# A hand-written order of instructions with longer due times for data that goes through DRAM, and a reordered opening

## The chip, the cores and the metric

The kernel runs on one core of one Trainium2 chip. The metric is the device time of one execution in microseconds (us), the median over the runs. A core has five engines with a stream of instructions each: PE (TensorE, matmuls), DVE (VectorE), ACT (ScalarE), POOL (GpSimd) and SP (SyncE, which here only issues DMAs). Each engine takes its instructions in the order of its stream and stops at one whose data is not there.

## The reference

One layer of a hybrid decoder for a prompt of 512 tokens and 8 sequences of 4 tokens (544 columns in all), model width 1024. Cut to what matters:

```python
mod = silu(c) @ w_ada + b_ada                    # adaLN: six vectors of 1024 per sequence
h = rmsnorm(x, mix_pre_g) * (1 + sc_m) + sh_m
p_rw, p_cv, p_gt = split(h @ w_in)               # 59 weight columns of 128
# RWKV-7: S_t = S_{t-1} diag(w_t) + S_{t-1} (-kk_t)(kk_t*a_t)^T + v_t k_t^T ;  y_t = S_t r_t
# convolution branch: GLU, depthwise conv (31 taps), layernorm, silu, w_conv_out
merged = sigmoid(g_a) * (y * g) @ w_o_rwkv + sigmoid(g_b) * y_b
x = x + gt_m * rmsnorm(merged @ w_out)
hf = rmsnorm(x) * (1 + sc_f) + sh_f              # then router, top 6 of 64 experts, shared expert
x = x + gt_f * rmsnorm(moe(hf))
```

## The kernel before

Activations stand transposed (128 channels by 544 tokens, eight such tiles). Float32 products are made from two fp32r parts: a weight column of 1024 x 128 is loaded, split by ACT (`wh`) and DVE (`wl`), and multiplied in 48 matmuls (eight channel tiles, three products, two halves of the tokens; line 611). `Stream` runs all columns of `w_in` one after the other in an order written by hand, with the convolutions among them, and then those of the two output projections. Each column's product lies in one of two PSUM tiles; column n waits until the output step of column n−2 has emptied its tile.

Around this stream run threads, each a Python generator: the opening, one for the adaLN rows, one for preparation and Gram matrices of the eight head pairs, the inverses, their assembly, the scan, the sample states. `Weave` puts them into one order: a thread yields an engine letter with an estimated duration, and an earliest start if it has one; the planner picks the next step by estimated time and priority and then emits its instructions. Nothing else decides the order on an engine. The estimates do not act on the chip: there an instruction waits only for its data. `arrival(mb)` is the planner's estimate for a transfer: 2 us, the megabytes at 0.36 MB/us behind earlier ones, and 1.2 us.

The places that matter here:

- Opening. `th_first` issues the loads on SP: c, all constants, x in two halves, sixteen adaLN weights of 0.52 MB with six buffers, the parameters among them, and at the end 2.2 MB of zeros into the accumulator `accs[1]`. `th_ada` multiplies each weight with silu(c) (line 468) and picks the rows by a second product (511). `th_ssq` squares x on ACT and sums over channels with 32 matmuls (526), then root and reciprocal (534). `th_h` makes xn, hf, hh and hl per channel tile; column 0 follows tile by tile, later columns come after it.
- adaLN rows (`th_rows`, line 1339 on). The other 32 weights come in pairs through two buffers; four weights are multiplied per PSUM bank while the lock `L` on two banks is held, which `sample`, `assemble` and `step` also take.
- Gram matrices (`gram`). For each head pair two halves: products on PE (995, 996), mask on DVE (1001) into `gm`, of which there is one buffer, six DMAs to DRAM. The transposes behind (1018) use the PSUM banks of the products. The step in question is

```python
            yield 'V', 1.37, max(t + .2, tv[-1] + 4. if c0 else 0)
            gm = rt([128, 4, 2, 2, 64], "gm", 1)
```

- Inverses. `th_inverse` solves 31 steps on DVE, writes the blocks to DRAM; `assemble` reads them back in another layout (`d1`, `gt`, `TT`) and multiplies (1195, 1208), then the scan of eight steps follows, for each of two groups of head pairs.
- After the columns of `w_in` and the scan: `th_yin` loads what the y stage needs, `th_y` normalises, `th_z`, router, experts.

Of the kernel before, what the change touches and what calls it, by code (L numbers as in the profile page):

```python
# [10 lines left out]
FT = mybir.dt.float32  # L11
# [3 lines left out]
OP = mybir.AluOpType  # L15
# [42 lines left out]
C_ID, C_MEAN, C_BLK, C_ONE, C_TRI = 0, 128, 256, 384, 512  # L58
C_HS = 640
C_SCAN = 642  # L60
# [6 lines left out]
C_SELC = C_SELR + 64  # L67
C_E64 = C_SELC + 9
C_EPS = C_E64 + 64
C_TOK = C_EPS + 2  # L70
# [285 lines left out]
def hybrid_kernel(ctx: ExitStack, tc: tile.TileContext, a, dbg=None, stop=None):  # L356
# [103 lines left out]
    x_in, c_done, r_done = events(2), Event(), Event()  # L460
    aw = {}
# [8 lines left out]
    def th_first():  # L470
        yield 'D', .5
        t = load(cT, a['cT'], .13)
        yield 'D', .5
        load(cst, a['const'][:, :C_END], .92)
        for s in (slice(0, 4), slice(4, 8)):
            yield 'D', .5
            x_in[s.start // 4].t = load(xT[:, s], a['xT'][:, s], 1.1)
        for i in range(16):
# [17 lines left out]
        load(accs[1][NP:], zt[:NS], .13)  # L496
# [19 lines left out]
    def th_ssq():  # L516
        ps = None
# [18 lines left out]

    def th_h(q):
        yield r_done
        for j in range(q, 8, 2):
            yield a_mod[8 + j]  # L540
            yield a_mod[j]
            yield 'V', .7
            V.tensor_scalar(A1[:, j, :], modT[:, 8 + j, :], 1.0, P_(P_G1, j), op0=OP.add, op1=OP.mult)
            xn = ap_.tile([128, T], FT, name="xn", tag=f"xn{q}", bufs=1)
            V.tensor_tensor(xn, xT[:, j, :], rstd, op=OP.mult)
# [16 lines left out]
    class Stream:  # L562
# [9 lines left out]
        def split(self):  # L572
            raw, at, m = {}, {}, 0
            ns = [n for n, c in enumerate(self.cols) if c[0] is not None]
            for i, n in enumerate(ns):
                while m < min(i + 2, len(ns)):
                    yield 'S', .4
# [1931 lines left out]
```

## Time and profile before

| | us |
|---|---|
| median of 3 runs | 1701.23 (1693.86 to 1704.89) |
| the profiled execution | 1702.24 |
| its span | 1700.4 |
| PE busy | 1500.6 (88%) |
| DVE busy | 692.7 (41%) |
| ACT busy | 525.8 (31%) |
| mean granted TensorE clock | 0.959 of full speed |

The page is read from the top: busy time of each engine, then the span in 40 slices, the chain of work that ended last, and the costliest groups of instructions with the idle time before them and what ended it. A busy PE is not PE at its peak. Idle time of an engine matters only where that engine sets the end of a stage, so the views are read stage by stage: busy times in windows, waits in a window, and the timeline.

### The profile page before, as it was taken

The numbers are of one execution on the slowest core, as the hardware profiler recorded it, in microseconds if no ns is written. First come the engines' busy times: TensorE is split into PE (matmuls) and PEld (weight loads), VectorE is DVE, ScalarE is ACT, GpSimd is POOL, SyncE is SP. The second block draws the span as 40 slices with busy tenths as digits, with TensorE's granted clock in tenths as the row PEclk, the third lists the DMA queues.
The fourth block names the chain that finished last, engine by engine and source line by source line (L and its number), as shares of the span: only waits on it lengthen the run. The fifth ranks groups of instructions, "written<-read, shape, count | busy, mean of one in ns | idle before, by whom it ended". The sixth has DMA issues, their size and how long they took to land.

```text
span 1700.4 us, 31359 instructions
## 1 busy us (share of the span) xinstructions
PE 1500.6 (88%) x12550; PEld 1071.6 (63%) x12550; DVE 692.7 (41%) x1633; ACT 525.8 (31%) x994; POOL 183.2 (11%) x171
## 2 busy tenths in 40 slices
PE   6889998988899987999999999999888898889891
PEld 4778777877787777998997774545433343333330
DVE  3527463577576675854553431212211111111113
ACT  4334342442354423561323512212111111111112
POOL 0000000000000000000000011223222222222211
PEclk9989999999799998999999999999999999999995
DMA  9786676558688687647625259999999999999997
GB/s 351 250 243 181 194 190 167 129 138 193 135 207 203 156 208 185 175 144 216 220 86 175 87 204 380 352 343 318 333 343 343 355 353 355 350 351 369 349 379 218
DMA packets 212328, 421.89 MB, mean 248 GB/s; under 512 B 95702, under 2 KB 135510, under 8 KB 186966
## 3 DMA queue, kind: packets, MB, share of 16 engines
q1 hardware_dynamic: 183926, 344.29, 62.5%
q10 hardware_dynamic: 17136, 46.60, 9.2%
q0 software_dynamic: 11120, 28.99, 7.4%
q8 instruction: 99, 1.62, 0.4%
q14 instruction: 47, 0.39, 0.1%
HBM read 359.20 MB, written 68.35 MB: 251 GB/s over the span
## 4 chain that ended last, share of the span: by engine, by line
PE 42%; issue 22%; DMA 15%; DVE 7%; POOL 6%; ACT 3%; SPq 3%; POOLq 0%; ACTq 0%; DVEq 0%
PE mm L611 18%; POOL acc L2192 3%; POOL xg L2187 3%; PE z L1631 3%; PE gu L2261 3%; PE ye L2268 2%; DMA wr<-in_w_in 2%; DMA im<-in_w_ada 2%; PE mm L805 2%; PE gu L2258 2%; DMA acc<-yo,tok 2%; DMA raw<-in_w_ex 2%; DMA imd<-gm 1%; SPq L445 1%; PE yt L1576 1%
## 5 line engine op out<-in xcount | busy, mean ns | idle before, releaser
L611 PE MATMUL mm<-hh,wh 128*128 128x272 f32 x944 | 224.6, 320 | 3.2 <-DVE gt L650 2.8
L611 PE MATMUL mm<-hl,wh 128*128 128x272 f32 x944 | 201.5, 296 | 0.8 <-DVE hl L556 0.8
L611 PE MATMUL mm<-hh,wl 128*128 128x272 f32 x944 | 200.2, 294 | 0.4 <-DVE wl L588 0.4
L611 PEld LDWEIGHTS mm<-hh,wh 128*128 128x128 f32 x944 | 155.2, 197 | 23.3 <-issue 17.1
L2261 PE MATMUL gu<-raw,xs 128*48 128x256 f32 (+2 forms) x1248 | 148.4, 386 | 22.6 <-DMA raw<-in_w_ex 18.9
L2304 DVE SCALAR_TENSOR_TENSOR hs<-hs,gate,gu 64x256 f32<-64x256 f32 (+6 forms) x65 | 30.7, 473 | 320.6 <-ACT hs L2302 320.6
L2268 PE MATMUL ye<-raw,ht 128*48 128x512 f32 (+6 forms) x440 | 139.8, 614 | 18.5 <-ACT ht L2311 15.0
L611 PEld LDWEIGHTS mm<-hl,wh 128*128 128x128 f32 x944 | 154.6, 196 | 1.3 <-DVE hl L556 1.2
L611 PEld LDWEIGHTS mm<-hh,wl 128*128 128x128 f32 x944 | 153.6, 196 | 0.7 <-DVE wl L588 0.7
L2258 PE MATMUL gu<-raw,xs 128*80 128x512 f32 (+3 forms) x304 | 136.4, 599 | 7.8 <-DMA raw<-in_w_ex 6.0
L2261 PEld LDWEIGHTS gu<-raw,xs 128*48 128x48 f32 (+2 forms) x1248 | 78.6, 125 | 92.9 <-DMA raw<-in_w_ex 25.1
L2192 POOL DMA_INDIRECT acc<-yo,tok x65 | 91.9, 1414 | 292.7 <-ACT yo L2331 253.1
L588 DVE TENSOR_TENSOR wl<-wr,wh 128x1024 fp32r<-128x1024 f32 x75 | 91.5, 1220 | 75.0 <-ACT wh L586 75.0
L2328 DVE COPY yo<-ye 64x512 f32<-64x512 f32 (+6 forms) x65 | 44.4, 684 | 185.6 <-PE ye L2268 165.4
L2302 ACT ACTIVATE hs<-gu 64x256 f32<-64x256 f32 (+6 forms) x65 | 24.7, 380 | 262.4 <-PE gu L2258 135.0
L2331 ACT ACTIVATE yo<-ye 64x512 f32<-64x512 f32 (+6 forms) x65 | 38.5, 593 | 213.1 <-DVE yo L2328 210.4
L2258 PEld LDWEIGHTS gu<-raw,xs 128*80 128x80 f32 (+3 forms) x304 | 48.4, 165 | 85.0 <-issue 68.2
L586 ACT ACTIVATE wh<-wr 128x1024 fp32r<-128x1024 f32 x75 | 79.5, 1059 | 50.8 <-PE mm L611 37.5
L2187 POOL DMA_INDIRECT xg<-td,tok x65 | 72.0, 1108 | 201.7 <-PE xgT L2247 187.2
L2268 PEld LDWEIGHTS ye<-raw,ht 128*48 128x48 f32 (+6 forms) x440 | 39.5, 139 | 78.6 <-issue 53.8
L805 PE MATMUL mm<-g,wdw 128*32 128x256 f32 x1024 | 58.6, 381 | 2.8 <-ACT dw L820 2.8
L1405 POOL MEMSET im<- 64x256 f32 x2 | 0.6, 307 | 495.2 <-DMA g<-gcd 327.7
(415 smaller groups left out, 2434.6 us busy)
## 6 DMA issues: line engine op xcount, KB each, us to landing
raw<-in_w_ex SPq DMA_DIRECT2D x168, 1024.0 KB, 9.8
wr<-in_w_in ACTq DMA_DIRECT2D x59, 512.0 KB, 5.2
tT<-in_w_ex SPq DMA_DIRECT2D x24, 1024.0 KB, 9.6
im<-in_w_ada SPq DMA_DIRECT2D x16, 1024.0 KB, 8.7
im<-imd SPq DMA_DIRECT2D x32, 512.0 KB, 6.9
g<-gcd SPq DMA_DIRECT2D x64, 142.0 KB, 5.3
aw<-in_w_ada SPq DMA_DIRECT2D x16, 512.0 KB, 5.6
gated<-gt ACTq DMA_DIRECT2D x16, 272.0 KB, 2.1
```

Of the source, the lines that this page charges most:

```text
L586: S.activation(hi, raw[i], AF.Copy)
L588: V.tensor_tensor(lo, raw[i], hi, op=OP.subtract)
L611: PE.matmul(ps[:, h, :H2], w[:, k, :], x[:, k, h * H2:(h + 1) * H2], start=(k == 0 and i == 0), stop=(k == KT - 1 and i == 2))
L805: PE.matmul(ps[32 * g:32 * g + 32, c, :256], w[:, b, g], x[:, g, 4 * b:4 * b + 256], start=(b == 0), stop=(b == 7))
L1631: PE.matmul(ps[:, h], m[:, k, OFF[tt]:OFF[tt] + 128], WO[w][:, k, 512 * h:512 * h + 512], start=(k == 0 and n == 0), stop=(k == KT - 1 and ...
L2187: G.indirect_dma_start(out=xg[:n], out_offset=None, in_=td, in_offset=bass.IndirectOffsetOnAxis(ap=col, axis=0), bounds_check=T - 1, oob_i ...
L2192: G.indirect_dma_start(out=accs[i], out_offset=bass.IndirectOffsetOnAxis(ap=col, axis=0), in_=ye[:n], in_offset=None, bounds_check=T - 1, ...
L2258: PE.matmul(pg[:n], x[:, k, :n], w, start=(k == 0), stop=(k == KT - 1))
L2261: PE.matmul(pg[p:p + n, :256], x[:, k, :n], w[:, c:c + 256], start=(k == 0), stop=(k == KT - 1))
L2268: PE.matmul(py[h], x[:, k, :n], w[:, 1024 * k + 512 * h:1024 * k + 512 * h + 512], start=(k == 0), stop=(k == 1))
L2328: V.tensor_copy(ye[:n, :512], py[0])
L2331: S.activation(ye[:n, 512:], py[1], AF.Copy)
```

## The change

Constants are laid out anew so that those of the opening (mean matrix, selection, epsilon) stand first; they are loaded alone, the rest after the tenth adaLN weight. The opening loads c and x first. Squares are made on ACT as before, but summed on DVE, and one product per half follows; xn is made in place on DVE in a thread of its own. The first two columns run together, tile by tile as h comes, each with its own PSUM tile; their output steps start when the opening's memory is released. The zeros go into the y stage, their memset from POOL to DVE. The planner's due times: second Gram mask 9 instead of 4 us after the first, assembly 6 us after the estimated arrival, row weights 3.5 us after it, with 0.65 instead of 0.85 us per product; loads of the first two column weights not before 14 us.

```diff
-C_ID, C_MEAN, C_BLK, C_ONE, C_TRI = 0, 128, 256, 384, 512
+C_MEAN, C_SELC, C_EPS, C_EARLY = 0, 128, 137, 144
+C_ID, C_BLK, C_ONE, C_TRI = (C_EARLY + 128 * i for i in range(4))
...
     def th_first():
         yield 'D', .5
         t = load(cT, a['cT'], .13)
-        yield 'D', .5
-        load(cst, a['const'][:, :C_END], .92)
         for s in (slice(0, 4), slice(4, 8)):
             yield 'D', .5
             x_in[s.start // 4].t = load(xT[:, s], a['xT'][:, s], 1.1)
+        yield 'D', .5
+        cst_in.t = load(cst[:, :C_EARLY], a['const'][:, :C_EARLY], .07)
+        yield 'D', .5
+        load(par, a['par'], .19)
+        W.spawn('first', th_silu(t), 4)
         for i in range(16):
...
             a_in[i].t = load(aw[i], a['w_ada'][AORD[i]], .52)
-            if i == 0:
-                yield 'S', .3, t
-                S.activation(cs, cT, AF.Silu)
-                fire(c_done)
-            if i == 1:
+            if i == 9:
                 yield 'D', .5
-                load(par, a['par'], .19)
-        zt = ap_.tile([128, D], FT, name="zeros")
-        yield 'G', .6
-        G.memset(zt, 0.0)
-        yield 'D', 1.
-        load(accs[1][:NP].rearrange("(i p) d -> p i d", p=128), zt[:, None].to_broadcast([128, 4, D]), 2.1)
-        load(accs[1][NP:], zt[:NS], .13)
+                load(cst[:, C_EARLY:], a['const'][:, C_EARLY:C_END], .85)
...
+    def th_sq():
         for j in range(8):
             yield x_in[j // 4]
-            yield 'S', .55
-            sq = ap_.tile([128, T], FT, name="sq", tag="sq", bufs=2)
-            S.activation(sq, xT[:, j, :], AF.Square)
-            yield 'P', .9
-            ps = ps or [bank([128, H2], "ssq") for _ in range(2)]
-            for h in range(2):
-                PE.matmul(ps[h], C_(C_MEAN, 128), sq[:, h * H2:(h + 1) * H2], start=(j == 0), stop=(j == 7))
+            yield 'S', .6
+            sqs[j] = ap_.tile([128, T], FT, name="sq", tag="sq" if j else "sum", bufs=3 if j else 1)
+            S.activation(sqs[j], xT[:, j, :], AF.Square)
+            fire(sq_in[j])
+
+    def th_ssq():
+        for j in range(8):
+            yield sq_in[j]
+            if j:
+                yield 'V', .72
+                V.tensor_tensor(sqs[0], sqs[0], sqs[j], op=OP.add)
...
+    def th_xn():
+        yield r_done
+        for j in range(8):
+            yield 'V', .72
+            V.tensor_tensor(xT[:, j], xT[:, j], rstd, op=OP.mult)
+            fire(xn_in[j])
...
                 while m < min(i + 2, len(ns)):
-                    yield 'S', .4
+                    yield 'S', .4, 14. if m < 2 else None
...
-                if i >= 2:
+                if i >= 3:
                     yield self.g[ns[i - 2]]
...
         def mm(self):
             for n, (src, ops, need, label, out) in enumerate(self.cols):
                 W.label(label)
+                if n == 1:
+                    continue
+                if not n:
+                    two = [n, n + 1]
+                    for i in two:
+                        yield self.s[i]
+                    ps = [mmtile() for _ in two]
+                    for k in range(KT):
+                        yield need[k]
+                        xh, xl = ops()
+                        for j in two:
+                            yield 'P', .76
...
+                    yield st_open
+                    for j in two:
+                        W.spawn(self.cols[j][3], self.cols[j][4](ps[j], self.e[j]), 3)
+                    continue
...
-            yield 'V', 1.37, max(t + .2, tv[-1] + 4. if c0 else 0)
+            yield 'V', 1.37, max(t + .2, tv[-1] + 9. if c0 else 0)
...
-        t = W.arrival(1.0)
+        t = W.arrival(1.0) + 6.
...
-                    yield 'P', .85, max(t, now())
+                    yield 'P', .65, max(t + 3.5, now())
...
         y_in.t = load(BR['XG'], xgd.rearrange("i p t -> p i t"), .56)
+        zt = yp.tile([128, D], FT, name="zeros")
+        yield 'V', 1.2
+        V.memset(zt, 0.0)
+        yield 'D', 1.
+        load(accs[1][:NP].rearrange("(i p) d -> p i d", p=128), zt[:, None].to_broadcast([128, 4, D]), 2.1)
+        load(accs[1][NP:], zt[:NS], .13)
...
-    W.run(h_done)
+    W.run([*h_done, gemms.g[1]])
```

## Rows read from the trace of the kernel before

**Rows 1.** Busy times in windows; columns: stretch, length, engines (instructions), clock, DMA share, GB/s.

```profile
58.00:740.00 682.00, 616.25 (x6918) 532.00 (x6915) 417.58 (x989) 270.91 (x508) 5.02 (x8) 0.94 0.71 180
...
775.00:900.00 125.00, 124.38 (x1069) 118.13 (x1069) 66.31 (x91) 32.24 (x37) 2.66 (x8) 0.99 0.54 168
...
1000.00:1600.00 600.00, 537.50 (x3048) 260.76 (x3046) 107.76 (x334) 114.25 (x247) 153.96 (x123) 0.99 1.01 349
```

**Rows 2.** PE's waits from 57 to 740: who waited for whom, us, times, longest.

```profile
PE bt L1018 <- DVE gm L1001: 24.4, 6, 6.9
PE pz L1195 <- DMA dx<-d1d: 15.4, 4, 7.7
PE rows L468 <- DMA im<-in_w_ada: 11.6, 5, 3.5
```

**Rows 3.** Busy times in windows after PE's stalls, and in one dense stretch.

```profile
86.10:92.30 6.20, 6.13 (x46) 4.44 (x46) 1.66 (x5) 2.55 (x5) 0.00 (x0) 0.50 1.08 232
...
440.10:454.20 14.10, 14.10 (x278) 13.16 (x280) 5.76 (x8) 1.77 (x3) 0.00 (x0) 0.50 0.42 69
...
817.00:890.00 73.00, 73.00 (x583) 72.88 (x582) 41.80 (x47) 24.97 (x27) 2.66 (x8) 1.00 0.48 155
```

**Rows 4.** PE's timeline in the first of these windows: start, us, instruction, count.

```profile
88.66 0.66 PE L611 MATMUL mm<-hl,wh 128*128 128x272 f32 x2
89.11 0.65 PE L611 MATMUL mm<-hh,wl 128*128 128x272 f32 x2
```

**Rows 5.** Timeline of the opening: reciprocal, last adaLN weight, ends of columns 0 and 1.

```profile
30.82 3.56 DVE L534 RECIPROCAL rstd<-rstd 128x272 f32<-128x272 f32 x2 [0.67 <-ACT rstd L530]
...
48.17 0.64 PE L468 MATMUL ada<-aw,cs 128*32 128x128 f32 x16
...
55.87 0.41 PE L611 MATMUL mm<-hh,wl 128*128 128x272 f32 x2
...
66.33 0.41 PE L611 MATMUL mm<-hh,wl 128*128 128x272 f32 x2
```

**Rows 6.** Busy times in a window of the opening.

```profile
4.00:30.00 26.00, 16.67 (x148) 12.16 (x152) 3.92 (x10) 9.65 (x18) 0.00 (x0) 1.00 1.02 418
```

**Rows 7.** Timeline of DVE and SP around two of eight pairs of Gram masks.

```profile
392.23 1.28 DVE L1001 TENSOR_TENSOR gm<-gram,cst 128x512 f32<-128x512 f32 x2
...
402.23 0.61 SPq L1009 DMA_DIRECT2D imd<-gm  x1
...
404.74 1.29 DVE L1001 TENSOR_TENSOR gm<-gram,cst 128x512 f32<-128x512 f32 x2 [7.45 <-DMA imd<-gm]
...
567.69 1.29 DVE L1001 TENSOR_TENSOR gm<-gram,cst 128x512 f32<-128x512 f32 x2 [0.15 <-PE gram L996]
...
575.11 1.29 DVE L1001 TENSOR_TENSOR gm<-gram,cst 128x512 f32<-128x512 f32 x2 [0.37 <-issue]
```

**Rows 8.** PE's timeline at the first assembly.

```profile
438.26 0.28 PE L1195 MATMUL pz<-dx,lx 32*32 32x32 f32 x2 [4.33 <-DMA dx<-d1d]
440.10 1.88 PE L1195 MATMUL pz<-dx,lx 32*32 32x32 f32 x62 [1.55 <-DMA dx<-d1d]
```

**Rows 9.** DMA issues from 0 to 60: count, KB each, us to landing.

```profile
acc<-zeros SPq DMA_DIRECT2D x1, 2048.0 KB, 10.3
```

**Rows 10.** DVE's timeline: a head pair's v done, its preparation's start; last Gram's end.

```profile
418.56 0.23 DVE L650 SCALAR_TENSOR_TENSOR v<-sh,par,v 128x8 f32<-128x8 f32 x1
...
420.37 0.50 DVE L890 TENSOR_SCALAR kn<-k,par 128x544 f32<-128x544 f32 x1
...
582.02 0.43 DVE L1039 TENSOR_TENSOR bonus<-half,v 128x272 f32<-128x272 f32 x1
```

**Rows 11.** Timeline at the stage's end: scan's last copy, last head norm, last gate's DMA.

```profile
737.10 0.38 ACT L1294 ACTIVATE ysb<-py 128x256 f32<-128x256 f32 x1 [2.34 <-PE py L1247]
...
755.44 0.69 DVE L1326 TENSOR_TENSOR ys<-ys,st 128x512 f32<-128x512 f32 x1
...
764.24 0.34 ACTq L690 DMA_DIRECT2D gated<-gt  x1
```

More of the change, by code (lines that the diff above doesn't have):

```diff
@@ L56 @@
 LOW = -3e38
-C_ID, C_MEAN, C_BLK, C_ONE, C_TRI = 0, 128, 256, 384, 512
-C_HS = 640
-C_SCAN = 642
+C_MEAN, C_SELC, C_EPS, C_EARLY = 0, 128, 137, 144
+C_ID, C_BLK, C_ONE, C_TRI = (C_EARLY + 128 * i for i in range(4))
+C_HS = C_TRI + 128
+C_SCAN = C_HS + 2
 C_MP = C_SCAN + T
@@ L66 @@
 C_SELR = C_LM + 1
[L67 to L70, printed above, removed]
+C_E64 = C_SELR + 64
+C_TOK = C_E64 + 64
 C_OV = C_TOK + 5
@@ L459, in hybrid_kernel @@
     a_in, a_out, a_mod, h_done = events(16), events(16), events(16), events(8)
-    x_in, c_done, r_done = events(2), Event(), Event()
-    aw = {}
+    x_in, c_done, r_done, cst_in, xn_in = events(2), Event(), Event(), Event(), events(8)
+    st_open, aw = Event(), {}
     rstd = ap_.tile([128, T], FT, name="rstd")
@@ L514, in th_ada @@
             fire(a_mod[n])
-    def th_ssq():
-        ps = None
+    sq_in, sqs = events(8), {}
+    def th_sq():
         for j in range(8):
             yield x_in[j // 4]
-            yield 'S', .55
-            sq = ap_.tile([128, T], FT, name="sq", tag="sq", bufs=2)
-            S.activation(sq, xT[:, j, :], AF.Square)
-            yield 'P', .9
-            ps = ps or [bank([128, H2], "ssq") for _ in range(2)]
-            for h in range(2):
-                PE.matmul(ps[h], C_(C_MEAN, 128), sq[:, h * H2:(h + 1) * H2], start=(j == 0), stop=(j == 7))
+            yield 'S', .6
[8 more added lines that the diff above has]
+                V.tensor_tensor(sqs[0], sqs[0], sqs[j], op=OP.add)
+        sum_ = sqs[0]
+        yield cst_in
+        yield 'P', 1.9
+        ps = [bank([128, H2], "ssq") for _ in range(2)]
+        for h in range(2):
+            PE.matmul(ps[h], C_(C_MEAN, 128), sum_[:, h * H2:(h + 1) * H2], start=True, stop=True)
         for h in range(2):
             s = slice(h * H2, (h + 1) * H2)
-            yield 'S', .4
+            yield 'S', .5, None, 'sqrt'
             S.activation(rstd[:, s], ps[h], AF.Sqrt, bias=C_(C_EPS, 1))
@@ L535, in th_ssq @@
         fire(r_done)
+    def th_xn():
[4 more added lines that the diff above has]
+            fire(xn_in[j])
     def th_h(q):
-        yield r_done
         for j in range(q, 8, 2):
+            yield xn_in[j]
             yield a_mod[8 + j]
             yield a_mod[j]
-            yield 'V', .7
+            yield 'V', .22
             V.tensor_scalar(A1[:, j, :], modT[:, 8 + j, :], 1.0, P_(P_G1, j), op0=OP.add, op1=OP.mult)
-            xn = ap_.tile([128, T], FT, name="xn", tag=f"xn{q}", bufs=1)
-            V.tensor_tensor(xn, xT[:, j, :], rstd, op=OP.mult)
+            xn = xT[:, j]
             yield 'S', .7
@@ L580, in split @@
                     m += 1
-                if i >= 2:
+                if i >= 3:
                     yield self.g[ns[i - 2]]
                 yield 'S', 1.05, at[i]
-                hi = wp.tile([128, KT, 128], FR, name="wh", tag="wh", bufs=2)
-                lo = wp.tile([128, KT, 128], FR, name="wl", tag="wl", bufs=2)
+                hi, lo = ((wp if i else ap_).tile([128, KT, 128], FR, name=w, tag=w, bufs=2 if i else 1) for w in ("wh", "wl"))
                 S.activation(hi, raw[i], AF.Copy)
@@ L594, in mm @@
                 W.label(label)
+                if n == 1:
[10 more added lines that the diff above has]
+                            yield 'P', .76
+                            wh, wl = self.hl[j]
+                            for i, (w, x) in enumerate(((wh, xh), (wh, xl), (wl, xh))):
+                                for h in range(2):
+                                    PE.matmul(ps[j][:, h, :H2], w[:, k, :], x[:, k, h * H2:(h + 1) * H2],
+                                              start=(k == 0 and i == 0), stop=(k == KT - 1 and i == 2))
+                    for j in two:
+                        fire(self.g[j])
+                    yield st_open
+                    for j in two:
+                        W.spawn(self.cols[j][3], self.cols[j][4](ps[j], self.e[j]), 3)
+                    continue
                 if src is None:
@@ L1766, in hybrid_kernel @@
         W.spawn('ada', th_ada(q), 2)
+    W.spawn('ssq', th_sq(), 4)
     W.spawn('ssq', th_ssq(), 3)
+    W.spawn('ssq', th_xn(), 0)
     for q in range(2):
@@ L1777, in hybrid_kernel @@
     cv['gg'] = cvp.tile([128, GW], FT, name="gg")
+    st_open.t = W.last
     G.memset(cv['gg'], 0.0)
```

5 lines of the change are left out of this document (4 added, 1 removed).

## The prediction, before the result

> **What bounds the kernel now.** I read the page's head and the busy times by stage first. The profiled execution took 1702.24 us, its span 1700.4, so 1.84 us lie around it; it stands 1.0 us above the median of the runs, 1701.23. By stage [rows 1]: from 58 to 740 us PE works 616.25 of 682 us at a mean granted clock of 0.94; from 775 to 900 it works 124.38 of 125; from 1000 to 1600 the DMA engines are busy all the time (share 1.01) and PE is not. So the expert stage is set by its weight transfers, which start when the router is done: what comes earlier before it moves the whole stage. What can be won there lies in the opening and in the 66 us that PE idles between 58 and 740.
>
> PE's waits by releaser over that stretch [rows 2] name three large ones: transposes behind the Gram mask on DVE, 24.4 us in 6 waits; assembly of the inverses behind a DMA, 15.4 in 4; the adaLN rows behind their weights, 11.6 in 5. That is 51.4 of the 66 us. These are the three places where the change raises the planner's due times. Each instruction stream is in order, so a wait that the planner does not foresee stops all later work of that engine, though the next weight column may be ready.
>
> A stall costs more than its length. After the ten longest the granted clock is 0.50, the 1.2 GHz level, for 2.8 to 14.1 us each, 53.8 us together (ten windows, the first and the longest shown [rows 3]). At that level two column matmuls start 0.45 us apart [rows 4], 227 ns each; in a stretch at 2.4 GHz, 583 matmuls take 73.00 us [rows 3], 125 ns each. So one us there loses 1 − 125/227 = 0.45 us, and the ten stretches 24 us.
>
> **The opening, part by part.** Before, x comes behind the 0.88 MB of constants, and the mean square is summed by 32 matmuls on PE between the adaLN matmuls; the second reciprocal ends at 34.4 [rows 5]. Then h is made, column 0 ends at 56.3 and column 1, 48 matmuls later, at 66.7 (start of the last pair plus 0.41) [rows 5]. Until then PE also did three groups of adaLN rows and one row product, 4 us: 62.7 net.
>
> After, the sum is made by DVE. x and cT (2.36 MB) stand first; at the 418 GB/s that the queues moved between 4 and 30 us [rows 6] they are in by about 9 us; squares, sum, two matmuls, two roots and the reciprocals (3.56 [rows 5]) then end near 20, an estimate; even at their old length, 22 us from x to the end of the reciprocals, they would end at 31. So the last adaLN weight decides. In front of it or among it: x and cT 2.36 MB, sixteen weights 8.39, constants 0.89, parameters and shift 0.31, four column weights 2.10: 14.0 MB. With 0.5 MB in by 4 us, (14.0 − 0.5)/0.418 + 4 = 36 us. From landing to the last h: before, from the last adaLN matmuls at 48.17 to the end of column 0 took 8.1 us [rows 5], other work between. I take 8: two columns end at 44. Both PSUM tiles are then full; column 2 waits for the first column's output step (about 3 us of ACT and DVE), so 47. Gain 62.7 − 47 = 15 us. Bounds: if PE stays at the low level, one pair of weights costs it 12 × 0.227 + 2 × 1.1 = 4.9 us while a pair arrives every 2.5, eight pairs from 20 us on end at 60: gain 0. If the output step hides behind row work: 18.
>
> The DMA page of the Trainium skill (DMA: Bandwidth & Descriptors, Where 436 GB/s comes from) holds that a core's loads from HBM end at about 358 GB/s. By it the last weight would land near 42 us and the gain would be 9. The row's 418 GB/s disagrees here, and the measurement decides.
>
> **The Gram mask.** The second mask of a pair reuses the tile of the first, whose six DMAs must have left. Planned distance between the starts is about 5.4 us (1.37 + 4), after the change 10.4. In the trace the eight distances run from 6.6 to 13.0; in the pair shown DVE waited 7.45 us, on an issue of 402.23, for a start at 404.74, 12.5 after the first [rows 7]. SP itself was late there. So five of eight fit the new plan and three are 2 us short. I take 18.4 of 24.4 as removed (bounds 10 and 24.4). What now runs in the gap is column work, whose splits stand behind the same DVE queue.
>
> **The assembly.** PE sat idle 4.33 + 1.55 us for the first inverse [rows 8] and 9.5 for the second. Six us more covers the first and leaves 3.5 of the second: 11.9 removed (bounds 6 and 15.4). The lock on the two PSUM banks is held through the wait, as it really was before.
>
> **The adaLN rows.** Longest wait 3.5 [rows 2], and 3.5 is what is added: all 11.6 go (bound 6, if the weights' transfer is later than now). The lock is held longer per group in the plan; the real transfer sets it today already.
>
> **Clock.** With the waits gone I refund the stretches behind the row waits (13.9 us), half of those behind the masks (9) and the first assembly (14.1): 37 × 0.45 = 16.6 (bounds 8 and 24).
>
> **The zeros.** 2.2 MB leave the opening; there they took 10.3 us from issue to landing [rows 9]. They go into the y stage, behind the first four y loads, on SP and on the same engines as the column weights. PE has 0.6 us idle in 125 there [rows 1], so no slack: between 0 and 10 us; I take 4, since a column's weight is asked for one column ahead. The memset moves from POOL to DVE, 1 to 1.2 us, under column work.
>
> **Two sums.** PE: 15 + 18.4 + 11.9 + 11.6 + 16.6 = 73.5. But the stage also ends with a chain: preparation, Gram, inverse, scan, head norms. Up to 420 us preparation starts when its columns come (v done 418.56, next start 420.37 [rows 10]); later each starts when the one before ends, the last at 582. The chain is moved by what PE gains before 420: 15 + 11.6 + 6 (clock of the rows) + 12.5 (four masks) + 2.5 (theirs) = 47.6, plus the first assembly's 5.9 + 6.3, less what three later masks are put back (10.4 against 8.8, 9.1 and 7.4 us [rows 7]): 6. That is 54. The scan's last copy at 737.1 [rows 11] would come at 683; the head norms follow, the last starting 18 us after the scan; the last gate leaves at 764.2 [rows 11]. With 20 us for them and their DMAs the stage cannot end before 703: 61 us. The smaller sum holds: 61, less 4 for the zeros and 4 for new waits: 53. 1702.24 − 53 = 1649 for such an execution, 1648 for the median.
>
> **Rivals.**
> (1) The opening pays, the rest hardly: new waits take the place of the old, because the transfers stay late by another name. For it: SP has one queue for all, and in the pair shown the last of the six issues itself came 10 us after the mask began [rows 7]. Against it: PE always has a next column. Gain 12 to 30: 1672 to 1690.
> (2) Nothing shows: the opening is held at the low clock (gain 0 to 5), the zeros take back up to 10, and the middle gives 5 to 15 against new waits of that size. The change then does not do what it says, since planned times are not times on the chip. For it speaks the lower bound of the opening. 1690 to 1712.
> (3) Slower: the chain becomes the bound through its planned lateness. Eight masks put back by 5 us and the assembly before the last scan by 6 are 46 us. If the columns finish early and the chain takes over none of their gain but the opening's, the scan ends at 737 + 46 − 15 = 768, and the 20 us of norms behind it have no cover: 788 against 764, so 1726. It decides from a net lateness of 7 us on (737 + 20 + 7 = 764). Against it: up to 420 us the preparations wait for columns [rows 10], so lateness there is absorbed, and in three of eight pairs the chip is already later than the new plan.
> (4) The norms are packed closer, the PE sum holds and what I left over goes too: 80 to 93, 1609 to 1622.
>
> **How the numbers follow.** The bounds of the terms add up to 0 + 10 + 6 + 6 + 8 − 10 = 20 at the low end and 18 + 24.4 + 15.4 + 11.6 + 24 = 93 at the high one: 1682 and 1609. Forecast (1622 to 1672) 0.57; rival 1, 0.20, of it 0.15 below 1684; rival 2, 0.10; rival 3, 0.07; rival 4, 0.06. One per cent, 17 us, is about what a measurement of this kernel tells from no change. Faster by more: 0.57 + 0.15 + 0.06 = 0.78; within: 0.05 + 0.10 = 0.15; slower: 0.07. The range 1615 to 1688 leaves out rival 3, nearly all of rival 2 and the tails of rivals 1 and 4; the likeliest one's own range is 1622 to 1672.
>
> **What would show it.** Right: columns 0 and 1 end near 44 us, the reciprocal near 20; PE's waits on mask, assembly and rows together under 15 us; the granted clock between the opening and the last gate near 0.98; last gate near 705 us; the y stage as full as now. Wrong: PE low through the whole opening; a new releaser with more than 20 us among PE's waits; PE idle behind the scan or head norms at the end of the stage; column weights late behind the zeros.

## The result, and the profile after

The changed kernel takes 1682.69 us (median of 6 runs, 1679.34 to 1684.10), the kernel before 1698.30 beside it (median of 6); the ratio is 0.9881, 95% interval 0.9855 to 0.9908. It is 1.2% faster by that ratio, which is the one on record and not the quotient of the two medians (0.9908, 15.6 us; for the runs below the two differ by up to 0.3%). The sign is the one forecast; the size, 53 us, is some three times too large. The profiled execution took 1684.10 us with a span of 1682.2.

Busy times by stage after the change, with the columns of [rows 1]:

```profile
58.00:740.00 682.00, 629.30 (x7024) 540.85 (x7023) 423.99 (x991) 268.19 (x504) 5.20 (x8) 0.95 0.71 182
775.00:900.00 125.00, 123.62 (x1003) 114.01 (x1004) 67.71 (x92) 35.09 (x47) 2.66 (x8) 1.00 0.57 184
1000.00:1600.00 600.00, 536.29 (x3079) 255.26 (x3079) 106.10 (x322) 117.62 (x253) 152.46 (x121) 0.99 1.01 351
```

The y stage is as full as before and the expert stage is still all DMA; the difference lies ahead of the z stage. In all 20 kernels profiled here the span less the time of the first z matmul is 801 to 810 us, so that matmul's start is a good measure of the change: 891.2 before, 875.4 after. PE alone up to there (stretch, length, busy, clock, DMA share, GB/s), before and then after:

```profile
0.00:891.20 891.20, 802.18 (x8652) 0.95 0.70 189
```

```profile
0.00:875.40 875.40, 798.66 (x8625) 0.94 0.71 193
```

The matmuls are the same but for 28 of the mean square (the counts are a record off). PE's idle time fell from 89.0 to 76.7 us and its busy time by 3.5: 12.3 + 3.5 = 15.8. The idle time is 12 us shorter, though PE's waits on mask and assembly alone are 22.5 shorter. PE's waits from 45 to 740 after the change, against [rows 2]:

```profile
PE bt L1054 <- DVE gm L1037: 16.4, 3, 10.8
PE rows L467 <- DMA im<-in_w_ada: 12.9, 4, 6.8
PE mm L841 <- ACT dw L856: 5.7, 2, 5.4
PE mm L647 <- DVE r L684: 2.8, 1, 2.8
PE half L931 <- DVE bonus L1075: 2.6, 1, 2.6
...
PE half L1073 <- ACT btv L1067: 1.8, 1, 1.8
...
PE pz L1231 <- DMA dx<-d1d: 0.9, 2, 0.5
```

The assembly's wait is gone (15.4 to 0.9), the mask's went from 24.4 to 16.4, of which one single wait is 10.8, and the rows' grew by 1.3. New ones stand between them: on a convolution's output step (`dw`), on the thread of preparations and Gram matrices (`bonus`, `btv`) and on column outputs (`r`, `XA`).

**The opening.** PE's groups up to the z stage that differ there (instructions | busy us, mean ns | idle before, releaser), before and after:

```profile
L468 PE MATMUL ada<-aw,cs 128*32 128x128 f32 x256 | 12.3, 332 | 4.2 <-DVE modT L513 2.8 <-DMA aw<-in_w_ada 1.4
L526 PE MATMUL ssq<-sq,cst 128*128 128x272 f32 x32 | 12.1, 519 | 11.9 <-ACT sq L522 11.9
```

```profile
L467 PE MATMUL ada<-aw,cs 128*32 128x128 f32 x256 | 12.8, 346 | 13.2 <-DMA aw<-in_w_ada 11.2 <-DVE modT L510 1.8
...
L534 PE MATMUL ssq<-sq,cst 128*128 128x272 f32 x4 | 2.2, 701 | 1.2 <-DVE sq L528 1.2
```

The mean square costs PE 9.9 us less work and 10.7 less waiting, and the first adaLN weight, now behind x, 9.8 more waiting. The timeline of that stretch, DVE, SP and PE:

```profile
16.07 3.55 DVE L542 RECIPROCAL rstd<-rstd 128x272 f32<-128x272 f32 x2
...
21.44 13.08 SPq L444 DMA_DIRECT2D aw<-in_w_ada  x6
...
44.21 0.65 PE L467 MATMUL ada<-aw,cs 128*32 128x128 f32 x16
...
49.95 0.41 PE L623 MATMUL mm<-hh,wl 128*128 128x272 f32 x2
...
53.55 0.49 PE L647 MATMUL mm<-hh,wh 128*128 128x272 f32 x2 [2.17 <-DVE XA L686]
```

Two columns end at 50.4 (49.95 + 0.41), where one ended at 56.3 and the second at 66.7 [rows 5]; column 2 starts at 53.55.

**The stage's end**, against [rows 11]: ACT's and DVE's timeline with the scan's last copy, the last gate's DMA and the last operation of the last head norm, then PE's first y work.

```profile
734.66 0.38 ACT L1330 ACTIVATE ysb<-py 128x256 f32<-128x256 f32 x1 [2.72 <-PE py L1283]
...
743.59 0.33 ACTq L726 DMA_DIRECT2D gated<-gt  x1
...
750.97 0.69 DVE L1362 TENSOR_TENSOR ys<-ys,st 128x512 f32<-128x512 f32 x1
```

```profile
758.41 1.87 PE L1603 MATMUL yt<-cst,yn 64*64 64x64 f32 x30 [4.08 <-DMA yn<-ysd]
```

The last gate leaves 20.6 us earlier, but the scan ends only 2.4 and the last norm 4.5 earlier. PE runs out of gate work, waits 4.1 us for the norm's output, and works at a mean clock of 0.53 from 757 to 768.

### The profile page after: what moved, and what is told of

It is laid out like the page before. It is cut to its first block, busy times and chain, and to the rows that moved or that the text cites. A ratio compares the mean times of both kernels' runs of the same rounds, so it can differ in the third digit from the quotient of the medians.

```text
span 1682.2 us, 31292 instructions
## 1 busy us (share of the span) xinstructions
PE 1495.6 (89%) x12522; PEld 1065.3 (63%) x12522; DVE 700.9 (42%) x1641; ACT 518.1 (31%) x987; POOL 182.2 (11%) x170
## 3 DMA queue, kind: packets, MB, share of 16 engines
q1 hardware_dynamic: 184070, 344.30, 62.7%
## 4 chain that ended last, share of the span: by engine, by line
PE 47%; DMA 36%; DVE 8%; ACT 4%; issue 3%; SPq 2%; ACTq 0%; POOLq 0%; DVEq 0%
DMA raw<-in_w_ex 23%; PE mm L647 18%; PE gu L2303 3%; PE ye L2313 3%; PE gu L2306 3%; PE z L1673 3%; PE mm L841 2%; DMA tT<-in_w_ex 2%; DMA wr<-in_w_in 2%; DVE wl L601 1%; DMA im<-in_w_ada 1%; PE yt L1618 1%; DMA acc<-yo,tok 1%; DVE dt L1190 1%; PE mm L623 1%
## 5 line engine op out<-in xcount | busy, mean ns | idle before, releaser
L647 PE MATMUL mm<-hh,wh 128*128 128x272 f32 x912 | 217.5, 321 | 4.9 <-DVE r L684 2.8
L647 PE MATMUL mm<-hh,wl 128*128 128x272 f32 x912 | 193.2, 294 | 0.4 <-DVE wl L601 0.4
L647 PE MATMUL mm<-hl,wh 128*128 128x272 f32 x912 | 193.6, 295 | 0.0
L2306 PE MATMUL gu<-raw,xs 128*48 128x256 f32 (+2 forms) x1248 | 148.9, 388 | 20.6 <-DMA raw<-in_w_ex 17.0
L647 PEld LDWEIGHTS mm<-hh,wh 128*128 128x128 f32 x912 | 149.5, 196 | 25.3 <-issue 15.4
L647 PEld LDWEIGHTS mm<-hl,wh 128*128 128x128 f32 x912 | 148.5, 195 | 0.0
L647 PEld LDWEIGHTS mm<-hh,wl 128*128 128x128 f32 x912 | 147.7, 195 | 0.6 <-DVE wl L601 0.6
```

The lines of the kernel that those rows point to most:

```text
L647: PE.matmul(ps[:, h, :H2], w[:, k, :], x[:, k, h * H2:(h + 1) * H2], start=(k == 0 and i == 0), stop=(k == KT - 1 and i == 2))
L2306: PE.matmul(pg[p:p + n, :256], x[:, k, :n], w[:, c:c + 256], start=(k == 0), stop=(k == KT - 1))
```

## The experiments

All times are device microseconds, each ratio against runs of the kernel before on the same chip (medians from 1698 to 1708), with its 95% interval. "z" is the start of the first z matmul in the profiled execution, "idle" and "busy" are PE's up to it. Read the table with the last group of runs in mind: edits that change no work moved the ratio by up to 0.008.

| kernel | median | ratio | interval | z | busy | idle |
|---|---|---|---|---|---|---|
| before | 1698.3 | 1 | | 891.2 | 802.2 | 89.0 |
| after | 1682.7 | 0.9881 | 0.9855 to 0.9908 | 875.4 | 798.7 | 76.7 |
| d_opening_only | 1703.6 | 0.9978 | 0.9959 to 0.9997 | 892.4 | 793.5 | 98.9 |
| e_due_only | 1701.9 | 0.9983 | 0.9948 to 1.0019 | 890.6 | 794.9 | 95.7 |
| g_open_asm | 1699.7 | 0.9977 | 0.9947 to 1.0006 | 888.2 | 793.7 | 94.5 |
| a_mask4 | 1685.6 | 0.9893 | 0.9833 to 0.9953 | 878.4 | 797.5 | 80.8 |
| b_asm0 | 1692.2 | 0.9925 | 0.9901 to 0.9948 | 879.4 | 792.6 | 86.8 |
| c_rows_old | 1686.2 | 0.9872 | 0.9828 to 0.9916 | 877.0 | 789.7 | 87.4 |
| i_short_inverse | 1696.0 | 0.9937 | 0.9904 to 0.9971 | 886.8 | 802.4 | 84.4 |
| k_prep_prio | 1711.9 | 1.0042 | 1.0011 to 1.0073 | 904.8 | 806.1 | 98.7 |
| n_norm3 | 1670.8 | 0.9798 | 0.9763 to 0.9833 | 863.9 | 792.2 | 71.7 |
| o_norm3_short | 1679.6 | 0.9865 | 0.9818 to 0.9912 | 867.9 | 785.1 | 82.7 |
| l_less_pe | 1700.5 | 0.9963 | 0.9939 to 0.9988 | 889.8 | 770.2 | 119.6 |
| p_before_norm3 | 1714.4 | 1.0058 | 1.0029 to 1.0087 | 907.4 | 804.8 | 102.5 |
| q_norm3_mask4 | 1687.5 | 0.9880 | 0.9837 to 0.9922 | 876.8 | 792.4 | 84.5 |
| t_norm1 | 1676.2 | 0.9814 | 0.9772 to 0.9856 | 870.3 | 795.1 | 75.2 |
| w_null_gram | 1684.8 | 0.9858 | 0.9817 to 0.9900 | 877.5 | 797.9 | 79.5 |
| x_null_split | 1680.9 | 0.9830 | 0.9784 to 0.9876 | 875.7 | 796.1 | 79.6 |
| y_before_split | 1723.0 | 1.0082 | 1.0046 to 1.0117 | 914.3 | 809.2 | 105.0 |
| z_before_gram | 1707.3 | 1.0011 | 0.9990 to 1.0031 | 896.0 | 799.9 | 96.1 |

### The change in halves: d_opening_only, e_due_only, g_open_asm

d is the changed kernel with the three due times of before; e is the kernel before with the three due times of after; g is d with the assembly's six microseconds.

```diff
# d: after, with          # e: before, with the reverse
-            yield 'V', 1.37, max(t + .2, tv[-1] + 9. if c0 else 0)
+            yield 'V', 1.37, max(t + .2, tv[-1] + 4. if c0 else 0)
-        t = W.arrival(1.0) + 6.
+        t = W.arrival(1.0)
-                    yield 'P', .65, max(t + 3.5, now())
+                    yield 'P', .85, max(t, now())
```

> The changed kernel with all three due times (mask, assembly, row weights) as before, so the new opening and the moved zeros alone. Theory C: PE's lead from the opening (v of the first head pair 26 us earlier) moves thread and columns together, 15 to 22 us under the kernel before. Rival P: the opening's 15 us less the idle at the start of the y stage, 5 to 12 us under the kernel before.

> The kernel before with the three later due times and nothing else. Theory C: PE waits less, but the thread is 40 to 55 us longer and starts where it did, so the scan ends at 755 to 775 and the stage later: 0 to 20 us over the kernel before. Rival P: PE's waits fall by some 30 us with their low clock, 25 to 40 us under the kernel before.

> The opening, the zeros and the assembly's six microseconds, with mask and row weights due as before. If mask and rows earn nothing (their waits stayed or were replaced), this is within 5 us of the changed kernel. Theory C: the thread is as short as in the kernel with the old mask time, so 0 to 8 us under the changed kernel. Rival P: 10 to 15 us over it.

Each half alone is worth 0.2%, together they are worth 1.2%. They were run in one order each, and the parts of the opening (the constants, the sum on DVE, two columns at once, the zeros) were not run one by one. In d the opening's lead is real at first (column v of pair 0 done at 100.1, before 114.5) and 2.5 us by pair 3 (297.0 against 299.5): PE waits 9.62 us for row weights at 88, and 30.4 us for the mask in all. In e the columns run 35 us ahead by the last pair (502.0 against 536.7), but that pair's preparation starts 9 us later (550.2 against 541.4), the scan ends 18 us later (755.5), and PE waits 12.0 us for the last norm at 775.9. This reads as if both PE's work and the chain held the stage, so that shortening one leaves the other; no run shows it directly. In g the assembly's six microseconds take PE's waits on the inverses from 15.4 us in d to 6.3, and z starts 4.2 us earlier, but the ratio stays (0.9977 against 0.9978).

### One due time back: a_mask4, b_asm0, c_rows_old

Each is the changed kernel with one of the three due times (mask, assembly, rows) as before.

> The changed kernel with only the second Gram mask due 4 us after the first again. Theory C (the thread of preparations and Gram matrices, now 460 us long instead of 405, sets the end of the scan and of the stage): the thread gets some 25 to 40 us shorter, the scan's last copy comes at 700 to 720 instead of 734.7, and the time is 5 to 15 us under that of the changed kernel although PE's waits behind the mask come back. Rival P (PE's own stalls set the time): six waits of 3 to 7 us with their stretches at the low clock come back, 15 to 25 us over the changed kernel.

> The changed kernel with the assembly due at the estimated arrival again. Both theories expect PE's two waits for the inverses' DMAs back, 12 to 15 us with their low clock, 20 in all. Theory C: these stop PE and the columns but hardly the thread, whose first group's stall lies in a preparation: scan end 3 to 8 us later, time 4 to 10 us over the changed kernel. Rival P: 15 to 20 us over it.

> The changed kernel with the row weights due at their estimated arrival again and 0.85 us per product. PE's waits on them were 11.6 us before and 12.9 after, so they were not removed: theory C and rival P both expect within 5 us of the changed kernel; if the lock held longer delays the sample states and through them the thread, 5 to 10 us under it.

The assembly's six microseconds make the largest step: without them the ratio is 0.9925, about 7 us worse, PE waits 9.4 us on the inverses again and 12.2 us for the last norm, and the scan ends at 742.8. The step is no larger than what a null edit moved the kernel before, so that they pay is likely and not shown. No gain shows for the rows' due time, nor for the mask's: without the latter the last bonus comes 18 us earlier (573.0 against 591.5), PE still waits for masks (15.9 us), the scan ends 4.5 us earlier and the time is the same. Yet g, which lacks both, is 1% slower than the changed kernel: what the due times earn does not add up from single runs. In a, d and e neither theory's forecast came true; b is what theory C gave, g near what rival P gave. The reason the rows still wait stands in the trace of the changed kernel, SP and PE:

```profile
67.17 17.42 SPq L444 DMA_DIRECT2D g<-gcd  x8
84.68 0.51 SPq L1430 DMA_DIRECT2D modd<-lx  x1
88.86 0.48 SPq L1389 DMA_DIRECT2D lx<-in_b_row  x1
89.44 1.05 SPq L444 DMA_DIRECT2D im<-in_w_ada  x2
...
94.89 1.94 PE L467 MATMUL rows<-im,cs 128*32 128x128 f32 x32 [6.80 <-DMA im<-in_w_ada]
```

The weights' issue stood on SP behind eight loads of the convolution that took the queue 17.4 us, and behind one more load, `lx`, that was issued 3.7 us after the store ahead of it had left SP. It was late at its issue, 5.5 us ahead of the matmul that PE stopped at; 3.5 us of planned lateness did not cover it. The one long mask wait is of the same kind, SP first, then DVE and PE:

```profile
513.50 0.61 SPq L1043 DMA_DIRECT2D imd<-gm  x1
...
521.42 0.57 SPq L1045 DMA_DIRECT2D imd<-gm  x1
...
525.99 1.29 DVE L1037 TENSOR_TENSOR gm<-gram,cst 128x512 f32<-128x512 f32 x2 [11.98 <-DMA imd<-gm]
...
526.82 1.08 PE L1054 MATMUL bt<-cst,BK 128*128 128x128 f32 x4 [10.84 <-DVE gm L1037]
```

The third of the six DMAs that free the mask's tile was issued 7.9 us after the second; the profile puts 7.2 of it down to a gate's DMA from another queue. Two windows at the low level, one in the opening, the other from inside this wait on:

```profile
20.10:33.80 13.70, 13.14 (x134) 10.85 (x126) 11.08 (x31) 7.13 (x14) 0.00 (x0) 0.50 1.02 418
...
518.40:532.10 13.70, 5.28 (x22) 3.92 (x24) 3.94 (x6) 2.29 (x6) 0.00 (x0) 0.50 0.58 148
```

### The chain alone: i_short_inverse, k_prep_prio

```diff
# i: after, with
-        for s in range(31):
+        for s in range(2 if g else 31):
# k: after, with
-    W.spawn('prep', th_prep(), 2)
+    W.spawn('prep', th_prep(), 6)
```

i leaves out 29 of the 31 substitution steps of the second group's inverse.

> The changed kernel with 2 of the 31 steps of the second group's inverse, the other 29 left out: the chain to the last scan is some 18 to 22 us shorter, PE's work is the same. Theory C: the scan's last copy comes 15 to 20 us earlier, the y stage starts 8 to 15 us earlier until PE's own work bounds it, and the time falls by as much. Rival P: 0 to 4 us.

> The changed kernel with the thread of preparations and Gram matrices at planner priority 6 instead of 2, so its steps go ahead of column work and output steps that could start up to 0.6 us earlier. Theory C: the thread shrinks from 500 us (first start to last end) by 15 to 40, the scan ends that much earlier and the time falls by 5 to 20 us. Rival P: no change or a loss of up to 10, since columns and their splits are put back.

Theory C failed in both runs, and rival P, which allowed 0 to 4 us of gain in i and up to 10 us of loss in k, was off too. In i the inverse ended 24 us earlier (599.5) and the scan 2 us later (736.7); the time rose by 9 us, which is within what a null edit moved. In k the last bonus came 41 us earlier (550.9), but the first group's scan was put off (its last copy at 636.9 instead of 545.4), the second's ended at 755.5, and the time rose by 1.6%. So in these orders the length of preparation, Gram and inverse did not by itself set the scan's end. A gap of 29 us between two outputs of i's scan (701.4 and 730.0) stands, 27 us long, in the kernel before too; its timeline there, DVE, ACT and SP:

```profile
696.91 0.68 DVE L1312 TENSOR_REDUCE st<-ysb 128x8 f32<-128x512 f32 x1
...
704.35 0.38 ACT L1294 ACTIVATE ysb<-py 128x256 f32<-128x256 f32 x1 [1.86 <-PE py L1247]
...
714.33 0.68 DVE L1315 TENSOR_TENSOR ysb<-ysb,st 128x512 f32<-128x512 f32 x1
...
728.72 0.36 SPq L1328 DMA_DIRECT2D ysd<-ysb  x1
...
731.25 0.38 ACT L1294 ACTIVATE ysb<-py 128x256 f32<-128x256 f32 x1 [1.48 <-DMA ysd<-ysb]
```

Step 6 of the scan may write its output tile only when the head norm of steps 2 and 3 has left it. That norm had its data at 687, made its first reduction on DVE at 696.9, went on from 714.3 among layer-norm work, since it is planned at priority 0, and left at 728.7. In the changed kernel such a gap, of 16 us, stands between steps 3 and 4 (697.4 and 713.7).

### Prompt head norms, and less work for PE: n_norm3, t_norm1, o_norm3_short, l_less_pe, p_before_norm3

```diff
# n: after, with (t: 1 instead of 3; o: n with i's edit; p: before with n's edit)
-                                       ysd[:, c - 1:c + 1, 4 * g:4 * g + 4], n), 0)
+                                       ysd[:, c - 1:c + 1, 4 * g:4 * g + 4], n), 3)
# l: after, with
-                        yield 'P', 0.8
+                        m = 2 if label == 'gate' else 3
+                        yield 'P', 0.8 * m / 3
-                        for i, (w, x) in enumerate(((wh, xh), (wh, xl), (wl, xh))):
+                        for i, (w, x) in enumerate(((wh, xh), (wh, xl), (wl, xh))[:m]):
```

> The changed kernel with one number different: the head norms that the scan starts are planned at priority 3, not 0. Theory N (the scan's last steps wait for head norms that are planned late: step 4 of the second group copies its output at 713.7, 16.3 us after step 3, where the steps before it are 7.5 apart): the steps of the second group stand 6 to 9 apart, the scan's last copy comes at about 726 instead of 734.7, the 4.1 us of PE idle at 758.4 for yn and most of the 10.2 us at half clock behind it go, and the time falls by 5 to 9 us against the changed kernel (about 0.983 of before). Theory P (PE's work plus the idle that the fixed order leaves sets the stage's end): the scan ends earlier, but the last gate does not, and the time stays within 4 us of the changed kernel (0.986 to 0.990).

> The changed kernel with the head norms at priority 1: the order differs in 57 lines on PE and 64 on DVE from the changed kernel's, all of it where norms stand. Theory N (norms planned late hold the second scan's last steps): the gap of 16.3 us between its steps 3 and 4 shortens, the scan ends 2 to 8 us earlier than 734.7, and the time falls by 2 to 8 us (0.983 to 0.987). Theory O (n_norm3's gain is another order's luck): no fall, 0.987 to 0.992.

> As the run before, and 29 of the 31 substitution steps of the second group's inverse are left out, as in i_short_inverse, so that the inverse ends 24 us earlier. There the scan still ended at 736.7, with a gap of 29 us between the outputs of its steps 5 and 6, where step 6 waits for the sixth head norm. Theory N: with prompt norms the scan ends at about 659 + 58 = 717, and the time is at or under that of n_norm3. Theory P: the scan ends early and nothing comes of it, since PE has the same matmuls before the y stage: within 5 us of i_short_inverse or of the changed kernel, whichever way the order falls (0.985 to 0.995).

> The changed kernel with the third of the three products (low half of the weights by the high half of the activations) left out in the 16 gate columns: 16 x 8 x 2 matmuls of 0.125 us in a dense stretch, 32 us of PE work less before the y stage, most of it from 590 to 740; no wait is touched. Theory P: the time falls by nearly all of it, 25 to 32 us (about 0.972 of before). Theory C (the chain preparation, Gram, inverse, scan sets the end): the scan still ends at about 735, PE idles for yn in front of the y stage, and the time falls by less than 8 us (0.984 or more).

> The kernel before with the head norms at priority 3. There step 6 of the second group copies its output at 731.2, 26.8 us after step 5, and the sixth norm, ready at 687, runs at 714.3. Theory N: the scan ends at about 717 instead of 737, and as it set the stage's end in the prediction's account, the time falls by 10 to 18 us. Theory P: the scan ends earlier, the last gate stays at about 764, and the time stays within 4 us of before.

With the norms prompt the changed kernel was faster in both orders tried. t, whose order hardly differs, ends its scan at 728.7 (6 us earlier), its last gate at 737.6 (6 earlier), and z starts 5.1 earlier. n is the fastest kernel of this study, 1670.75 us, 0.9798 of before, with an interval that lies below the changed kernel's; it reaches into that of x_null_split below (0.9784 to 0.9876), so that the norms pay is likely and not shown. Its scan ends at 729.0, not 726; PE still waits 6.7 us for yn, which was expected to go; what fell is busy time, 6.5 us (the clock's mean up to z is 0.96 against 0.94), and 5 us of idle:

```profile
0.00:863.90 863.90, 792.20 (x8625) 0.96 0.72 195
```

With the norms prompt the short inverse does let the scan end early (o, which leaves out the same 29 steps as i: 714.7), and y starts at 739.3, but PE had waited 16.0 us for a weight's split at 626 and z starts 4 us later than n's. So in this order a shorter chain did not give an earlier z.

l leaves out the third product of the 16 gate columns. It has 28.5 us less PE work than the changed kernel, no due time was touched, and it is 0.8% slower. The loss is no larger than what a null edit moved; that nothing near 28.5 us was won is beyond it:

```profile
0.00:889.80 889.80, 770.16 (x8368) 0.93 0.70 189
```

```profile
627.19 0.82 PE L648 MATMUL mm<-hh,wh 128*128 128x272 f32 x2 [12.32 <-ACT wh L599]
...
771.64 0.59 PE L1604 MATMUL yt<-cst,yn 64*64 64x64 f32 x6 [14.92 <-DMA yn<-ysd]
```

The gates, now cheaper in the plan, were ordered ahead of the chain: the last leaves at 685.1 (743.6 in after), the inverse ends at 643.6 (623.3), the scan at 756.8, where PE has little else to do. PE idles 43 us more. The largest part is none of these: 20.9 us in two waits for a weight's split on ACT (12.3 us of it at 627), where the changed kernel has no such wait, and 15.3 us are waits for the last norm in front of the y stage (4.1 there). The theory that PE's work alone sets the time falls. The other has the idle PE in front of the y stage right, but not that the scan would keep its place. Since the edit also lowers the planned cost of a gate, the order changed with the work; the same work taken out at the old planned cost was not run, so the two are not separated. And p shows that the norms' priority is no rule: on the kernel before it moved the last bonus from 582 to 624.8, and the ratio is 1.0058, less than a null edit's 1.0082 there.

### The thread again, and edits that mean nothing: q_norm3_mask4, w_null_gram, x_null_split, y_before_split, z_before_gram

q is n_norm3 with the mask's due time at +4. The others change one planned cost and no work: a Gram half 1.95 to 1.85 (w on after, z on before), a subtraction on DVE 1.2 to 1.15 (x on after, y on before).

> n_norm3 with the second Gram mask's due time back at +4. Theory T (the preparation and Gram thread is paid for once prompt norms no longer hold the scan): the last bonus comes about 20 us before n_norm3's 598.1, the second group's inverse ends at about 606 and its scan at about 712, and the time is 5 to 12 us under n_norm3 (0.973 to 0.977 of before). Theory P (PE's work and its idle set the end): PE waits for gm again, the time is that of n_norm3 within 4 us or longer (0.978 to 0.990).

> The changed kernel with the planned cost of a Gram half on PE at 1.85 us, not 1.95: no work, wait or due time differs, only the order that the plan writes (about a third of PE's lines move by a few places). Theory O (the order alone moves the time by several us): 5 to 15 us away from the changed kernel, to either side. Theory S (the order is steady, and differences of 5 us between these kernels mean their edits): within 3 us of it (0.986 to 0.990).

> The changed kernel with the planned cost of one subtraction on DVE, the low half of a column's weights, at 1.15 us, not 1.2: a second order for the same work. Theory O: 5 to 15 us away from the changed kernel, to either side, and not where w_null_gram is. Theory S: within 3 us of it.

> The kernel before with the null edit of x_null_split (1.15 us for 1.2 in the plan, the same work). Theory O (the order alone moves the time by several us): 3 to 12 us away from before, to either side. Theory S: within 3 us of before. Either way the change itself is real if this stays above 0.994 of before, since the changed kernel in its three orders stands between 0.983 and 0.988.

> The kernel before with the null edit of w_null_gram (1.85 us for 1.95 in the plan). The same expectations as y_before_split: 3 to 12 us away by theory O, within 3 us by theory S.

q is slower than n (z 12.9 us later, masks cost PE 26.5 us, 9.3 in n): with the norms moved, the mask's distance seems worth having, though the step of 0.8% is again the size of a null edit. The thread's length is not tested by it: the last bonus came 7 us earlier, not 20. The null edits moved the changed kernel by −0.2 and −0.5%, the kernel before by +0.8 and +0.1%. So 2 to 14 us between two of these kernels need no cause but the order that the plan wrote, and a, c, w, x and after can't be ranked. The readings of b, i, o, p and q above, and l's loss, rest on steps of that size too. The change itself stands above that: three orders of before lie at 1, 1.0011 and 1.0082, three of after at 0.9881, 0.9858 and 0.9830. Their means, 1.0031 and 0.9856, give 0.9826, some 30 us; the 16 us of the pair compared are at the low side of it. In the traces of the same three orders each, z starts 24 us earlier on the mean (900.5 to 876.2), of it 18 us idle and 6 busy. PE's idle time by what it was about to write, means of the three orders before and after: mask (`bt`) 26.6 and 12.6, assembly (`pz`) 15.6 and 0.5, rows 13.6 and 13.1; against it the norms' output (`yt`) 4.0 and 10.2, `half` 0.2 and 4.9, `mean` 1.1 and 3.1.

## Why the prediction was right or wrong

**The step that failed.** The forecast is the smaller of two sums, and both rest on the step that time taken from a wait is kept by what stands behind it. The chain's sum puts the scan's last copy 54 us earlier; it came 2.4 us earlier (734.7), and the last gate 20.6 instead of 61. PE's sum is 73.5 us; PE came to the z stage 15.8 us earlier. Of the 41.9 us of waits on mask, assembly and rows that were to go, 21.2 went in this pair of orders (29.6 on the mean of three); 15 us of new waits came where 4 were allowed. Of the signs named, the three waits together stand at 30.2 us (under 15), the clock from 58 to 740 at 0.95 (near 0.98), the last gate at 743.6 (near 705). The measured time lies inside the stated range of 1615 to 1688, but by its width: the likeliest case's own range, 1622 to 1672, is missed. The terms one by one:

**Right.** The sign, and the stage that moves. The reciprocal ends at 19.6 (about 20). The queues move 417 GB/s between 4 and 30 us, 418 before [rows 6]. (By the Trainium skill's DMA: Bandwidth & Descriptors, Where 436 GB/s comes from, it would be about 358; the changed kernel's trace disagrees as the one before did.) The assembly: 14.5 of 15.4 us gone, 11.9 forecast, and gone in all three orders; that it paid in time b_asm0 makes likely, g does not show. The zeros: issued at 767, 14.7 us to land instead of 10.3 [rows 9]; the y stage has 123.62 busy of 125 against 124.38, so under 1 us instead of the 4 taken, inside the bounds of 0 to 10.

**The opening: 44, measured 50.4.** What failed is that the last adaLN weight is in when 14.0 MB are in. Windows of the changed kernel, then the same opening in d, and its last adaLN issues on SP and last column pair on PE:

```profile
4.00:36.00 32.00, 21.23 (x228) 17.36 (x229) 22.02 (x48) 17.65 (x33) 0.00 (x0) 0.79 1.02 409
36.00:44.00 8.00, 8.00 (x108) 6.74 (x106) 4.45 (x14) 4.34 (x10) 0.00 (x0) 1.00 1.02 293
```

```profile
20.10:33.80 13.70, 13.27 (x150) 11.16 (x145) 11.06 (x31) 7.13 (x14) 0.00 (x0) 1.00 1.02 415
...
21.78 12.46 SPq L444 DMA_DIRECT2D aw<-in_w_ada  x6
...
49.66 0.41 PE L623 MATMUL mm<-hh,wl 128*128 128x272 f32 x2
```

By 36 us the queues had moved 13.7 MB (0.6 in the first 4 us, then 409 GB/s), as forecast, but the last weight was not among them. Its issue left SP at 34.5, since SP had to wait for PE to free one of the six buffers (15.2 us in 7 waits up to 36), and its matmuls began at 44.2; from 36 to 44 us the DMA engines were busy all the time (share 1.02) but moved 293 GB/s, with row weights of 1 MB issued behind it. That these slowed it was not tested. The bound named for gain 0, PE at the low level, is not what held it: PE was at that level from 20.1 to 33.8 here, but at 1.00 in d, where the last issue left at 34.2 and the columns ended at 50.1 all the same. Column 2 starts at 53.55, not 47, so by the prediction's own account (62.7 net) the gain is 9 us, not 15. What the step did not ask is what the lead is worth later: in d most of it is lost by pair 3.

**The mask: 18.4 of 24.4, measured 8** (14 of 26.6 on the mean of three orders). A planned distance did not make SP's six DMAs prompt when other transfers hold its queue: four of eight distances in the trace of after are over the planned 10.4 by more than 1 us (11.9, 13.7, 14.8 and 22.4).

**The rows: all 11.6 gone, measured 1.3 more.** The bound "if the weights' transfer is later than now" was the case at the longest wait: the issue stands behind SP's loads. It was named as a bound, then not weighed.

**The clock: a refund of 16.6, not seen.** Without the mean square's 9.9 us PE's busy time should have fallen by 9.9 and by the refund, and fell by 3.5. The stretches at 0.50 up to the z stage sum to 99.0 us in the trace's clock records, 88.7 before, and PE's busy time inside them to 81.1 and 72.0; at the prediction's 0.45 us lost per us that is 4.1 of the missing 6.4, an estimate, and the rest stays open. One trace does not settle the sign: in the null orders the sums are 78.5 and 75.1 after the change, 112.6 and 95.6 before. What was wrong is to tie the low level to the waits removed. It does not even follow the sum of idle time: d idles 98.9 us and is low for 81.9, the changed kernel 76.7 and 99.0.

**New waits: 4 us, measured 15** (PE's groups dw, half, pt, mean, the other columns and yt: 11.4 us before, 26.4 after). The forecast gave no reason for its 4.

**The chain account: scan at 683, measured 734.7.** Three things in it were wrong. The preparations did not start with their columns: the lead at column v of the last pair was 43.8 us (492.9 against 536.7), yet its preparation started at 541.4 in both kernels, since from the first preparation's start it took 451.7 us instead of 425.6. "Three later masks, 6 us" was too small: from a pair's preparation to its last bonus the eight pairs sum to 460 us, 405 before. And the scan's end was taken to follow the inverse; in i it did not, and the gap in its steps ends with the DMA of a head norm that was planned last.

**Rival 1** came nearest (1672 to 1690): new waits in the place of old ones, because transfers stay late by another name, SP's single queue among them. It was given 0.20, the likeliest case 0.57. Its other half, that the opening pays by itself, d does not show (0.9978). **Rival 3** names what e's trace has: the columns early, the chain late, PE idle in front of the y stage; but e is not slower than before, and why the whole change fares better is not shown.

What stays open: why the order after the change has its idle time where it has. The runs show that it moves with edits that mean nothing, not a rule by which it moves.

## What to carry to other kernels

In a kernel whose in-order streams are written by a planner, add up the whole ledger before taking credit for a wait: PE's work plus all its idle time up to the next bound. Here 21 us went from three kinds of wait and 15 us came back in others. Ask of a late transfer whether it is late in flight or late at its issue; here a due time a few us later did not cover the second. And before an effect of 1% is put down to an edit, change one planned cost by a few per cent on both kernels and see how far the time moves; compare several orders of each.

## What the runs showed that was not expected

Taking 28.5 us of matmuls off PE, with their planned cost, won nothing: the kernel was 0.8% slower (l_less_pe), with 43 us more idle time. The same opening ran at 0.50 from 20.1 to 33.8 in one kernel and at 1.00 in another, and its columns ended 0.3 us apart. A null edit of 0.05 us in the plan moved the kernel before by 0.8%, 18 us by the medians. A head norm of a few us of work, most of it run 27 us after its data came, held two scan steps that had nothing to do with its values, through the buffer it had still to leave.
